# Projections of the second layer dealt as one stream over the token groups, and their weight preparation moved to ScalarE and GpSimd

## The chip, the cores and the metric

One NeuronCore of one Trainium2 chip. The metric is device time in microseconds (us) of the whole kernel. The kernel before takes 2705.66 us (median of three runs, 2705.16 to 2706.25). The engines are TensorE (PE for its matmuls, PEld for its weight loads), VectorE (DVE), ScalarE (ACT), GpSimd (POOL) and the queue of SyncE that issues the DMAs (SP).

## The reference, cut to what matters

Two layers over a sequence of 2048 tokens, 1024 features. The first is a gated linear attention. The second, which the change touches, is a stick-breaking attention of 16 heads of 64:

```
hk = rms_norm(x, kv_gain) * (1 + kv_scale) + kv_shift;  k, v = split(hk @ w_kv)
h  = rms_norm(x, gain)    * (1 + scale)    + shift;     q, g = split(h @ w_in)
z = q k^T * 64^-0.5                       # for each head, s < t only
log_beta = log_sigmoid(z);  log_one_minus = log_beta - z
w = exp(log_beta + reverse_cumsum(log_one_minus) - log_one_minus)
x = x + gate * ((w @ v) * silu(g)) @ w_out;   y = rms_norm(x, final_gain)
```

The norm's scale `a` and shift `b` are not applied to the tokens. They go into the weights: the projection uses `a * W` (one factor for each input feature) and adds the bias `b @ W`.

## The kernel before, in words

The sequence is cut into 4 token groups `g` of 512, the 16 heads into 8 pairs `p`. The normalised tokens lie in DRAM as a rounded part and a remainder (`xn_d`), and every product of the projections is three matmuls of 512 columns: high weight by high token, high by low, low by high (`mm3`, L143 to L153; the matmuls are L150, L151, L152).

**Projections.** `pair_linear(p, g)` (L732) computes v, k, q and the gate for one pair and one group, in this order. It is a generator: each `yield` follows the three matmuls of one of 8 slices of the features, so it has 4 times 8 steps and one more for its tail (`LIN_STEPS = 33`). It begins by loading eight tiles `xb` on SP. After each product ACT and DVE take the result out of PSUM.

**Weights.** `load_scaled` (L121) prepares a weight of 1024 by 256 in eight slices of 128 by 256, `kt` = 0 to 7. For each slice ACT writes the rounded `a * raw` (`hi`, L132), DVE the remainder (`lo`, L133), and DVE adds `b * raw` to a sum (`acc`, L138 for the first slice, L140 for the rest) from which TensorE later makes the bias (`pair_bias`, L720). A pair has two such weights, `w_kv` and `w_qg`, so 16 slices. `relaxed(n)` gives an instruction a priority that is n places later. The raw halves have three buffers, the prepared halves ten.

**Attention.** A `Unit` is one head, one query group and one key chunk of 512. It has four steps. `scores` makes z on TensorE (L821, L822), takes the sigmoid on ACT (L825) and runs the product scan on DVE (L830); in a chunk on the diagonal POOL first masks the last 128 columns (L827). `turn`, five steps later, transposes on TensorE (L838, four times) and splits into `sh` on ACT (L841) and `sl` on DVE (L842). `values`, some two steps after that, multiplies by v (L855, L856). Group g has 2(g+1) units, so 8, 16, 24 and 32 steps for g = 0 to 3.

**Order.** TensorE's order is that of the program text. The other engines' queues are put in order when the program is built, by a planner that takes ready instructions by priority. The loop of `layer1` (L964 on) runs the attention of one (pair, group) and fills each step with other work, by `step` (L956): during group g all 33 steps of the projection of group g+1, whatever g is; during group 3 those of the next pair's group 0. The weights `w_kv` of the next pair are dealt to the second half of group 2, `w_qg` to the first 60% of group 3. During group 3 of the last pair the fill is the final output projection.

The z banks and the transpose banks in PSUM are two each; the pool `m2` of 128 by 512 tiles (S, sh, sl and others) has 22 buffers, the token tiles 12.

Of the kernel before, what the change touches and what calls it, by code (L numbers as in the profile page):

```python
# [9 lines left out]
F32 = mybir.dt.float32  # L10
F32R = mybir.dt.float32r
AF = mybir.ActivationFunctionType
ALU = mybir.AluOpType
# [3 lines left out]
P = 128  # L17
D = 1024
KT = D // P
SEQ = 2048  # L20
TG = 512
NG = SEQ // TG
GH = 4
GV = 256
SBP = 8
# [9 lines left out]
def yoco_kernel(ctx: ExitStack, tc: tile.TileContext, I: dict, O: dict):  # L35
# [6 lines left out]
    nc = tc.nc  # L42
# [3 lines left out]
    wraw = ctx.enter_context(tc.tile_pool(name="wraw", bufs=3))  # L46
    wsp = ctx.enter_context(tc.tile_pool(name="wsp", bufs=10))
    m4 = ctx.enter_context(tc.tile_pool(name="m4", bufs=14))
    m2 = ctx.enter_context(tc.tile_pool(name="m2", bufs=22))
    pl = ctx.enter_context(tc.tile_pool(name="pl", bufs=4, space=PSUM))  # L50
    pz = ctx.enter_context(tc.tile_pool(name="pz", bufs=2, space=PSUM))
    pw = ctx.enter_context(tc.tile_pool(name="pw", bufs=2, space=PSUM))
# [3 lines left out]
    def t2(name, dt=F32):  # L56
        return m2.tile([P, TG], dt, tag="m2", name=name)
# [7 lines left out]
    def bank(pool, name):  # L65
# [9 lines left out]
                            fill=0.0, base=0, channel_multiplier=1)  # L75
# [45 lines left out]
    def load_scaled(name, src, out, mod, acc):  # L121


        a, b = mod
        for hf in range(2):
            raw, hi, lo = load_half(name, src, hf)
            out += [(hi[:, j], lo[:, j]) for j in range(4)]
            for j in range(4):
                kt = 4 * hf + j
                s = a[:, kt:kt + 1]  # L130
                with relaxed(100):
                    nc.scalar.activation(hi[:, j], raw[:, j], AF.Copy, scale=s)  # L132
                    nc.vector.scalar_tensor_tensor(lo[:, j], raw[:, j], s, hi[:, j].bitcast(F32),  # L133
                                                 op0=ALU.mult, op1=ALU.subtract)
                s = b[:, kt:kt + 1]
                with relaxed(400):
                    if kt == 0:
                        nc.vector.tensor_scalar(acc, raw[:, j], s, None, op0=ALU.mult)  # L138
                    else:
                        nc.vector.scalar_tensor_tensor(acc, raw[:, j], s, acc, op0=ALU.mult, op1=ALU.add)  # L140
                yield

    def mm3(out, w, blk, x, order=range(KT), first=True, last=True):  # L143
# [15 lines left out]
    def relaxed(n):  # L159

        return tc.high_priority(offset=-n) if n else nullcontext()
# [8 lines left out]
    def run(gen):  # L170
        for _ in gen:
            pass
# [535 lines left out]
    def new_weights(p):  # L708
        W = Piece()
        W.acc = t2(f"wacc_{p}").rearrange("p (i f) -> p i f", i=2)  # L710
        W.w, W.bias = {}, [None, None]
        return W

    def pair_weights(p, W, i):

        which, m = (("w_kv", "kvm"), ("w_qg", "l1m"))[i]
        W.w[which] = []
        return load_scaled(f"{which}{p}", I[which][p], W.w[which], mods[m], W.acc[:, i])
# [11 lines left out]
    LIN_STEPS = 4 * KT + 1  # L730
# [191 lines left out]

    LAG_T, LAG_V = 5, 2

    Ws = {}

    def prepare_pair(p):
# [4 lines left out]
    def layer1(after):  # L932
        Ls = {p: [] for p in range(SBP)}
        weave(pair_linear(0, 0, Ws[0], Ls[0]), (after, 0, 2))
        turns, values = [], []
        def final_all():

            seq = [final(g) for g in range(NG - 1)]
            seq += [final(NG - 1, i * TG // 2, TG // 2) for i in range(2)]
            for i, gen in enumerate(seq):  # L940
                ahead = final_inputs(i + 1) if i + 1 < NG else iter(())
                if i == 0:
                    yield from final_inputs(0)
                for j in range(FINAL_STEPS):
                    next(gen)
                    if i and j == (8 if i < 4 else 14):
                        run(seq[i - 1])
                    if j >= 32 and j % 4 == 0:
                        next(ahead, None)
                    yield  # L950
                run(ahead)
            run(seq[-1])

        finals = final_all()

        def step(gens, at):  # L956
            for f in gens:
                gen, n, f0, f1 = f[:4]
                want = min(n, int(n * (at - f0) / (f1 - f0) + 1e-6))
                while f[4] < want:  # L960
                    next(gen, None)
                    f[4] += 1

        for p in range(SBP):  # L964
            for g in range(NG):
                units = []
                for h in range(2):
                    before = None
                    for c in range(g, -1, -1):
                        before = Unit(p, g, h, c, Ls[p], before)  # L970
                        units.append(before)

                fill = [[after, 26, 0, 1, 0]] if p == 0 and g < 2 else []
                if p == SBP - 1 and g + 1 == NG:
                    fill.append([finals, FINAL_STEPS + SBP - 1, 0, 1.0, 0])
                elif g + 1 < NG:
                    fill.append([pair_linear(p, g + 1, Ws[p], Ls[p]), LIN_STEPS, 0, 1, 0])
                elif p + 1 < SBP:
                    fill.append([pair_weights(p + 1, Ws[p + 1], 1), KT, 0, 0.6, 0])
                    fill.append([pair_linear(p + 1, 0, Ws[p + 1], Ls[p + 1]), LIN_STEPS, 0, 1, 0])  # L980
                if g == 2 and p + 1 < SBP:
                    Ws[p + 1] = new_weights(p + 1)
                    fill.append([pair_weights(p + 1, Ws[p + 1], 0), KT, 0.5, 1, 0])
                steps = [(u, j) for u in units for j in range(4)]
                for i, (u, j) in enumerate(steps):
                    u.scores(j)
                    turns.append((u, j))
                    step(fill, (i + 0.7) / len(steps))
                    if len(values) > LAG_V:
                        v = values.pop(0)  # L990
                        v[0].values(v[1])
                    step(fill, (i + 1) / len(steps))
                    if len(turns) > LAG_T:
                        t = turns.pop(0)
                        t[0].turn(t[1])
                        values.append(t)
                for f in fill:
                    if f[0] is not finals and (f[0] is not after or g):
                        run(f[0])
        while turns or values:  # L1000
            for _ in range(3):
                next(finals)
            if turns:
                t = turns.pop(0)
                t[0].turn(t[1])
                values.append(t)
            for _ in range(3):
                next(finals)
            if len(values) > (LAG_V if turns else 0):
                v = values.pop(0)  # L1010
                v[0].values(v[1])
        run(finals)

    last = []
    play(layer0())
    layer1(last[0])


# [54 lines left out]
```

## Time and profile before

| | |
|---|---|
| median of three runs | 2705.66 us (2705.16 to 2706.25) |
| the profiled execution, its own time | 2703.88 us |
| its span, first to last instruction | 2702.1 us |
| PE busy | 2607.2 us, 96% |
| DVE busy | 2110.4 us, 78% |
| ACT busy | 1517.6 us, 56% |
| POOL busy | 167.4 us, 6% |
| mean granted TensorE clock | 0.989 of full |

Busy time is a union over the span, with issue and semaphore instructions left out. Matmuls overlap one another, so a matmul's duration is longer than the distance to the next one. The attention of the second layer begins at 976 us; pair 1 lies between 1170.5 and 1363.6 us, with its groups beginning at 1170.5, 1202.4, 1242.0 and 1296.8 us.

### The profile page before, as it was taken

The page shows a single profiled execution, that of the slowest core. Times are in us where ns is not written, and L with a number is a line of the kernel's source. Part 1 is how long each engine was busy: PE and PEld are TensorE (multiplying, and loading weights), DVE is VectorE, ACT ScalarE, POOL GpSimd, SP SyncE. Part 2 cuts the span into 40 slices and gives each one's busy share as a digit, 9 for nine tenths or more (in the row PEclk, how much of TensorE's full clock was granted, in tenths as well). Part 3 has the DMA queues.
Part 4 walks back from the last instruction along what each step waited for, and adds up shares of the span by engine and source line. Part 5 has one row for each costly group of instructions (what it writes and reads, how often), then busy time and mean ns, then how long its engine had stood idle before and what let it go on. Part 6 is the DMA issues. An engine that isn't in the chain of part 4 may idle for free.

```text
span 2702.1 us, 38165 instructions
## 1 busy us (share of the span) xinstructions
PE 2607.2 (96%) x14040; PEld 2184.4 (81%) x14040; DVE 2110.4 (78%) x2933; ACT 1517.6 (56%) x2677; POOL 167.4 (6%) x358
## 2 busy tenths in 40 slices
PE   5999999999999999999999999999999999999998
PEld 4888888888788878788787887887887887887887
DVE  7647767676675658978979969979879789789866
ACT  4746756574485445545545645546556555556644
POOL 3000000000000011000010010010000010010000
PEclk7999999999999999999999999999999999999999
DMA  6326445545732463342243334243243243323464
GB/s 246 118 74 209 151 151 175 168 148 173 232 131 72 164 247 127 106 145 90 96 146 116 114 107 154 88 137 116 75 148 110 72 151 113 115 93 117 148 212 147
DMA packets 116682, 371.91 MB, mean 138 GB/s; under 512 B 13872, under 2 KB 18096, under 8 KB 116496
## 3 DMA queue, kind: packets, MB, share of 16 engines
q1 hardware_dynamic: 116496, 369.47, 40.8%
q8 instruction: 111, 1.82, 0.3%
q14 instruction: 75, 0.61, 0.1%
HBM read 311.75 MB, written 40.89 MB: 131 GB/s over the span
## 4 chain that ended last, share of the span: by engine, by line
PE 75%; DVE 17%; ACT 3%; issue 3%; DMA 1%; POOL 0%; SPq 0%; DVEq 0%; POOLq 0%; ACTq 0%
PE pt L838 7%; DVE S L830 5%; PE z L822 4%; PE o L856 4%; PE z L821 4%; PE o L855 3%; DVE sl L842 3%; PE pg L150 2%; PE pg L152 2%; PE pg L151 2%; PE pf L150 2%; PE pf L151 2%; PE pf L152 2%; PE py L150 2%; PE lk L150 2%
## 5 line engine op out<-in xcount | busy, mean ns | idle before, releaser
L841 ACT ACTIVATE sh<-pt 128x512 fp32r<-128x512 f32 (+3 forms) x640 | 341.5, 534 | 531.7 <-PE pt L838 522.1
L842 DVE SCALAR_TENSOR_TENSOR sl<-pt,sh 128x512 fp32r<-128x512 f32 (+3 forms) x640 | 384.0, 601 | 163.5 <-ACT sh L841 157.6
L830 DVE TENSOR_TENSOR_SCAN S<-S,S 128x512 f32<-128x512 f32 x384 | 489.5, 1275 | 3.4 <-ACT S L825 3.0
L838 PE MATMUL pt<-ident,S 128*128 128x128 f32 x2176 | 346.9, 275 | 34.7 <-DVE sl L842 34.2
L838 PEld LDWEIGHTS pt<-ident,S 128*128 128x128 f32 x2176 | 266.1, 141 | 119.7 <-DVE sl L842 33.0
L825 ACT ACTIVATE S<-z 128x512 f32<-128x512 f32 (+3 forms) x640 | 339.5, 531 | 12.6 <-PE o L856 4.6
L821 PE MATMUL z<-k,q 128*128 128x512 f32 (+3 forms) x640 | 284.4, 444 | 0.0
L822 PE MATMUL z<-k,ql 128*128 128x512 f32 (+3 forms) x640 | 234.1, 366 | 0.9 <-DVE sl L842 0.5
L856 PE MATMUL o<-sl,v 128*128 128x512 f32 (+3 forms) x640 | 234.2, 366 | 0.0
L855 PE MATMUL o<-sh,v 128*128 128x512 f32 (+3 forms) x640 | 230.6, 360 | 0.0
L830 DVE TENSOR_TENSOR_SCAN S<-S 128x128 f32<-128x128 f32 (+3 forms) x256 | 209.3, 820 | 19.7 <-POOL S L827 16.7
L827 POOL TENSOR_SCALAR_AFFINE_SELECT S<-S 128x128 f32<-128x128 f32 x256 | 86.1, 337 | 1251.1 <-ACT S L825 1232.2
L444 PE MATMUL pv<-wh_v,h 128*128 128x256 f32 x512 | 155.0, 303 | 0.0
L446 PE MATMUL pv<-wh_v,h 128*128 128x256 f32 x512 | 145.3, 284 | 0.0
L445 PE MATMUL pv<-wl_v,h 128*128 128x256 f32 x512 | 145.2, 284 | 0.0
L855 PEld LDWEIGHTS o<-sh,v 128*128 128x128 f32 x640 | 120.6, 188 | 27.2
L856 PEld LDWEIGHTS o<-sl,v 128*128 128x128 f32 x640 | 120.6, 189 | 25.7
L821 PEld LDWEIGHTS z<-k,q 128*128 128x128 f32 x640 | 121.8, 190 | 5.5
L822 PEld LDWEIGHTS z<-k,ql 128*128 128x128 f32 x640 | 123.1, 192 | 1.5 <-DVE sl L842 0.7
L150 PE MATMUL pg<-h,wh_g 128*128 128x512 f32 x256 | 112.6, 440 | 0.0
L150 PE MATMUL lk<-xb,wh_w_kv 128*128 128x512 f32 x256 | 102.5, 400 | 7.6 <-DVE oB L869 7.6
L150 PE MATMUL lv<-xb,wh_w_kv 128*128 128x512 f32 x256 | 102.9, 402 | 3.5 <-DMA xb<-xn 3.5
(266 smaller groups left out, 6350.3 us busy)
## 6 DMA issues: line engine op xcount, KB each, us to landing
xb<-xn SPq DMA_DIRECT2D x256, 512.0 KB, 5.0
wa_l<-in_w_ada_dram SPq DMA_DIRECT2D x40, 512.0 KB, 5.2
wr_f<-in_w_out_dram SPq DMA_DIRECT2D x40, 512.0 KB, 3.8
x<-in_x_dram SPq DMA_DIRECT2D x32, 512.0 KB, 6.5
wr_v<-in_w_v_dram SPq DMA_DIRECT2D x32, 512.0 KB, 4.5
wr_kq<-in_w_kq_dram SPq DMA_DIRECT2D x32, 512.0 KB, 4.1
wr_g<-in_w_g_dram SPq DMA_DIRECT2D x32, 512.0 KB, 3.9
wr_out<-in_w_out_dram SPq DMA_DIRECT2D x32, 512.0 KB, 3.8
```

Of the source, the lines that this page charges most:

```text
L150: nc.tensor.matmul(out, hi, x[kt][0], start=first and i == 0, stop=False)
L444: nc.tensor.matmul(o, xh, hi, start=i == 0, stop=False)
L446: nc.tensor.matmul(o, xl, hi, start=False, stop=i == len(steps) - 1)
L821: nc.tensor.matmul(z, L.q[:, h, tcol], k[:, h, 0:w], start=True, stop=False)
L822: nc.tensor.matmul(z, L.ql[h][:, tcol], k[:, h, 0:w], start=False, stop=True)
L825: nc.scalar.activation(s, z, AF.Sigmoid, scale=-SCALE_B)
L830: nc.vector.tensor_tensor_scan(s[:, ::-1], s[:, ::-1], s[:, ::-1], 1.0 if diag else self.before.S[tb][:, 0:1], ALU.mult, ALU.min)
L838: nc.tensor.transpose(pt[:, tb * P:(tb + 1) * P], self.S[tb][:, sb * P:(sb + 1) * P], ident)
L841: nc.scalar.activation(hi, pt[:, t0 * P:], AF.Copy, bias=-1.0)
L842: nc.vector.scalar_tensor_tensor(lo, pt[:, t0 * P:], -1.0, hi.bitcast(F32), op0=ALU.add, op1=ALU.subtract)
L855: nc.tensor.matmul(o, v, hi, start=self.diag and sb == 0, stop=False)
L856: nc.tensor.matmul(o, v, lo, start=False, stop=self.c == 0 and sb == 3)
```

## The change

Two things change. The projections of all pairs become one generator, `projections()`, which the attention steps draw from by a running count `made`. At the end of group g of pair p the count must have reached `33 * (4p + g + 1)`, as before, and is let run ahead by `AHEAD[g]` of a projection; within a group the steps are dealt evenly. The weights of the next pair are drawn by every second step of the stream: `w_kv` from the middle of the projection (p, 3), `w_qg` from the start of (p+1, 0). In `load_scaled` all DVE instructions are gone: POOL makes the bias sum with a multiplication and an addition, ACT also scales the raw slice in place, and POOL subtracts. `m2` has one buffer less, and POOL gets two of 128 by 256.

```diff
-    m2 = ctx.enter_context(tc.tile_pool(name="m2", bufs=22))
+    m2 = ctx.enter_context(tc.tile_pool(name="m2", bufs=21))
+    wtmp = ctx.enter_context(tc.tile_pool(name="wtmp", bufs=2))
...
-                s = a[:, kt:kt + 1]
-                with relaxed(100):
-                    nc.scalar.activation(hi[:, j], raw[:, j], AF.Copy, scale=s)
-                    nc.vector.scalar_tensor_tensor(lo[:, j], raw[:, j], s, hi[:, j].bitcast(F32),
-                                                 op0=ALU.mult, op1=ALU.subtract)
-                s = b[:, kt:kt + 1]
                 with relaxed(400):
                     if kt == 0:
-                        nc.vector.tensor_scalar(acc, raw[:, j], s, None, op0=ALU.mult)
+                        nc.gpsimd.tensor_scalar(acc, raw[:, j], b[:, kt:kt + 1], None, op0=ALU.mult)
                     else:
-                        nc.vector.scalar_tensor_tensor(acc, raw[:, j], s, acc, op0=ALU.mult, op1=ALU.add)
+                        t = wtmp.tile([P, 256], F32, tag="wtmp", name=f"wt_{name}_{kt}")
+                        nc.gpsimd.tensor_scalar(t, raw[:, j], b[:, kt:kt + 1], None, op0=ALU.mult)
+                        nc.gpsimd.tensor_tensor(acc, acc, t, op=ALU.add)
+                with relaxed(100):
+                    s = a[:, kt:kt + 1]
+                    nc.scalar.activation(hi[:, j], raw[:, j], AF.Copy, scale=s)
+                    nc.scalar.activation(raw[:, j], raw[:, j], AF.Copy, scale=s)
+                    nc.gpsimd.tensor_tensor(lo[:, j], raw[:, j], hi[:, j].bitcast(F32), op=ALU.subtract)
                 yield
...
+    AHEAD = (0.1, 0.0, 0.15, 0.6)
...
+        def projections():
+            for p in range(SBP):
+                for g in range(NG):
+                    side, start, every = iter(()), 0, 2
+                    if g == 0:
+                        if p == 0:
+                            continue
+                        side = pair_weights(p, Ws[p], 1)
+                    elif g == NG - 1 and p + 1 < SBP:
+                        Ws[p + 1] = new_weights(p + 1)
+                        side, start = pair_weights(p + 1, Ws[p + 1], 0), LIN_STEPS // 2
+                    for i, _ in enumerate(pair_linear(p, g, Ws[p], Ls[p])):
+                        if i >= start and (i - start) % every == 0:
+                            next(side, None)
+                        yield
+                    run(side)
+                    yield
+        stream = projections()
+        made = [0]
+        def project(n):
+            while made[0] < n and next(stream, 0) is None:
+                made[0] += 1
...
-                elif g + 1 < NG:
-                    fill.append([pair_linear(p, g + 1, Ws[p], Ls[p]), LIN_STEPS, 0, 1, 0])
-                elif p + 1 < SBP:
-                    fill.append([pair_weights(p + 1, Ws[p + 1], 1), KT, 0, 0.6, 0])
-                    fill.append([pair_linear(p + 1, 0, Ws[p + 1], Ls[p + 1]), LIN_STEPS, 0, 1, 0])
-                if g == 2 and p + 1 < SBP:
-                    Ws[p + 1] = new_weights(p + 1)
-                    fill.append([pair_weights(p + 1, Ws[p + 1], 0), KT, 0.5, 1, 0])
+                n0, n1 = made[0], int(LIN_STEPS * (NG * p + g + 1 + AHEAD[g]))
                 steps = [(u, j) for u in units for j in range(4)]
+                def go(at):
+                    step(fill, at)
+                    project(n0 + int(at * (n1 - n0) + 1e-6))
                 for i, (u, j) in enumerate(steps):
...
-                    step(fill, (i + 0.7) / len(steps))
+                    go((i + 0.7) / len(steps))
...
-                    step(fill, (i + 1) / len(steps))
+                    go((i + 1) / len(steps))
...
+                project(LIN_STEPS * (NG * p + g + 1))
```

## Rows read from the trace of the kernel before

**Rows 1.** The page: busy time of engines, and the chain that ended last, by engine.
```profile
PE 2607.2 (96%) x14040; PEld 2184.4 (81%) x14040; DVE 2110.4 (78%) x2933; ACT 1517.6 (56%) x2677; POOL 167.4 (6%) x358
...
PE 75%; DVE 17%; ACT 3%; issue 3%; DMA 1%; POOL 0%; SPq 0%; DVEq 0%; POOLq 0%; ACTq 0%
```
**Rows 2.** Windows, pairs 1 and 6 and the end: stretch, length, busy of PE, PEld, DVE, ACT, POOL.
```profile
1170.50:1363.60 193.10, 187.83 (x1003) 155.50 (x1001) 166.50 (x235) 106.89 (x213) 15.04 (x40) 1.00 0.35 115
...
2136.00:2328.80 192.80, 187.83 (x1003) 155.54 (x1002) 166.25 (x232) 106.33 (x210) 16.09 (x40) 1.00 0.36 118
...
2456.70:2702.00 245.30, 229.82 (x1252) 196.24 (x1250) 190.98 (x264) 127.79 (x197) 4.47 (x8) 0.98 0.48 159
```
**Rows 3.** Windows, groups 0 to 3 of pair 1.
```profile
1170.50:1202.40 31.90, 31.90 (x164) 26.57 (x162) 17.68 (x25) 11.97 (x24) 3.70 (x10) 1.00 0.25 71
1202.40:1242.00 39.60, 39.60 (x213) 33.25 (x212) 32.26 (x44) 20.39 (x41) 4.06 (x10) 1.00 0.49 168
1242.00:1296.80 54.80, 51.96 (x281) 42.41 (x279) 51.72 (x81) 34.84 (x71) 3.71 (x10) 1.00 0.34 113
1296.80:1363.60 66.80, 64.36 (x354) 53.28 (x353) 64.84 (x88) 39.69 (x78) 3.57 (x10) 1.00 0.31 107
```
**Rows 4.** Windows, pair 1: the stretch of its weight preparation, and one behind it.
```profile
1260.00:1304.00 44.00, 39.86 (x212) 31.47 (x211) 43.66 (x73) 27.20 (x57) 2.39 (x7) 1.00 0.45 150
...
1318.00:1364.00 46.00, 46.00 (x259) 38.82 (x258) 44.18 (x56) 28.58 (x55) 2.07 (x6) 1.00 0.30 98
```
**Rows 5.** Waits of PE, from 1260 to 1304 us: total us, times, longest.
```profile
PE pt L838 <- DVE sl L842: 4.1, 7, 1.2
```
**Rows 6.** Waits of PE, pair 0 (976 to 1170.5 us): total us, times, longest.
```profile
PE pt L838 <- DVE sl L842: 4.0, 7, 1.2
PE lv L150 <- DMA xb<-xn: 3.5, 1, 3.5
PE lk L150 <- DVE oB L869: 1.1, 1, 1.1
```
**Rows 7.** Groups by line, 1260 to 1304 us: count, busy us, mean ns, idle before.
```profile
L830 DVE TENSOR_TENSOR_SCAN S<-S,S 128x512 f32<-128x512 f32 x12 | 15.3, 1272 | 0.0
L842 DVE SCALAR_TENSOR_TENSOR sl<-pt,sh 128x512 fp32r<-128x512 f32 (+3 forms) x18 | 10.8, 597 | 0.1
...
L133 DVE SCALAR_TENSOR_TENSOR wl_w_qg<-wr_w_qg,a_l,wh_w_qg 128x256 fp32r<-128x256 f32 x8 | 3.7, 471 | 0.0
```
**Rows 8.** Windows, 1260 to 1304 us, the instructions on the bias sum alone.
```profile
1260.00:1304.00 44.00, 0.00 (x0) 0.00 (x0) 6.94 (x16) 1.00 0.45 150
```
**Rows 9.** Weight preparation by line, whole span: ns min/median/max.
```profile
L132 ACT ACTIVATE wh_w_kv<-wr_w_kv,a_kv x64: 493/500/512, 911.9 to 2227.8; 128x256 fp32r<-128x256 f32 x64
...
L133 DVE SCALAR_TENSOR_TENSOR wl_w_kv<-wr_w_kv,a_kv,wh_w_kv x64: 452/464/480, 914.2 to 2230.3; 128x256 fp32r<-128x256 f32 x64
...
L140 DVE SCALAR_TENSOR_TENSOR wacc<-wr_w_kv,cond_kv,wacc x56: 454/469/486, 918.3 to 2249.9; 128x256 f32<-128x256 f32 x56
```
**Rows 10.** Timeline: three projection matmuls lie between these two starts.
```profile
1320.27 0.40 PE L150 MATMUL lk<-xb,wh_w_kv 128*128 128x512 f32 x1
...
1320.97 0.28 PE L855 MATMUL o<-sh,v 128*128 128x256 f32 x1
```
**Rows 11.** POOL, and DVE beside it, by line: ns min/median/max, first and last start.
```profile
L323 POOL TENSOR_TENSOR x<-x,r_x x8: 1714/2240/2248, 20.5 to 35.4; 128x512 f32<-128x512 f32 x8
...
L341 POOL TENSOR_SCALAR xn<-x,a_l,cond_l x4: 1188/1718/2076, 44.2 to 49.2; 128x512 f32<-128x512 f32 x4
...
L827 POOL TENSOR_SCALAR_AFFINE_SELECT S<-S x256: 291/295/1894, 977.4 to 2511.5; 128x128 f32<-128x128 f32 x128
...
L482 POOL TENSOR_SCALAR_AFFINE_SELECT sc<-sc x16: 637/638/1620, 88.8 to 877.9; 128x512 f32<-128x512 f32 x16
...
L244 DVE SCALAR_TENSOR_TENSOR aa_l<-wa_l,s_col,aa_l x35: 1273/1285/2177, 12.0 to 726.0; 128x1024 f32<-128x1024 f32 x35
```
**Rows 12.** Waits of SP's queue in pair 1: total us, times, longest.
```profile
SPq L106 <- DVE wacc L140: 22.2, 2, 16.4
```

## The prediction

> **What bounds the kernel now.** I read the page first. TensorE is 96% busy and holds 75% of the chain, VectorE holds 17% [rows 1]. That is a mean, so I cut the second layer into its pairs. Pair 1 lasts 193.1 us, and TensorE is busy in 187.83 of them; pair 6 is 192.8 with the same 187.83, and the four between are as pair 1 within 0.1 us [rows 2]. So a pair has 5.27 us in which TensorE stands still. No re-dealing of TensorE's own work can give more than that, as long as its matmuls cost what they cost.
>
> Then the groups. In groups 0 and 1 TensorE is never idle and VectorE is busy for 17.7 of 31.9 and 32.3 of 39.6 us. In groups 2 and 3 TensorE loses 2.84 and 2.44 us and VectorE is 94% and 97% busy [rows 3]. The idle time lies in one place: from 1260 to 1304 us VectorE works 43.66 of 44 us and TensorE 39.86; from 1318 to 1364 TensorE works all 46 us while VectorE, at 96%, just keeps up [rows 4]. In the first stretch TensorE waits seven times for `sl`, 4.1 us [rows 5]. What sets that stretch apart is the weights: the bias sum takes 6.94 us there [rows 8] and the eight remainders of `w_qg` 3.7 [rows 7]. So the bound is TensorE nearly everywhere, and VectorE for some 44 us of each pair, because the weights of the next pair are prepared on it.
>
> **The change, part by part.** *The stream.* Three projection matmuls take 1320.97 - 1320.27 = 0.70 us [rows 10], so the 33 steps of a projection take 23.1 us. Taken from TensorE's busy time in rows 3, attention alone is 8.8, 16.5, 28.9 and 41.3 us for groups 0 to 3. The new counts follow from 33(4p+g+1+AHEAD): 17, 30, 37 and 48 steps, 132 as before. Group times with TensorE full: 8.8+11.9 = 20.7, 16.5+21.0 = 37.5, 28.9+25.9 = 54.8, 41.3+33.6 = 74.9; in all 187.9 us. The stream by itself removes no work. It makes groups 0 and 1 shorter and group 3 longer, so that VectorE has more TensorE time beside it where it was late.
>
> *Weights off VectorE.* A pair loses 16 remainders of 0.46 to 0.47 us and 16 sums of about 0.47 [rows 9]: 15.0 us. VectorE's 166.5 us [rows 2] become 151.5 of 187.9.
>
> *Weights on POOL.* 16 multiplications, 14 additions and 16 subtractions of 128x256 for a pair. No row shows these at that width. The nearest with two inputs is 128x512: beside it a VectorE sum of 1285 ns takes up to 2177, so POOL held it up by 0.89 us [rows 11]. The mask takes 295 ns for 128 columns and 638 for 512, so some 409 or 0.64 of the latter for 256 [rows 11]; I take 0.64 x 0.89 = 0.57 us (bounds 0.45, half, and 0.89, all of it). For the multiplication with one input I take the mask's 0.41 (upper bound half of the fastest 1188 ns, 0.59). Sum 16 x 0.41 + 30 x 0.57 = 23.7 us, on an engine that is busy 15.0 of 193 us [rows 2].
>
> *What POOL does to VectorE.* The scan reads SBUF twice and takes 1272 ns; `sl` (full width some 0.68, mean of all forms 597 ns) reads its main input from PSUM [rows 7]. POOL's own mask took up to 1894 ns instead of 295 [rows 11]. So I count that a POOL instruction waits for a running scan, and then holds up the next. If two of them (0.41 + 0.57) start as a scan ends, `sl` covers 0.68 of it and the next scan is 0.30 us late: 0.15 for each, 7 us for 46. Bounds: 0 (all under `sl`) and 23.7 (all in front of a scan).
>
> Is there room? The stretch of rows 4 has 18 steps [rows 7]. Of VectorE's 43.66 us at most 43.66 - 6.94 - 3.7 = 33.0 stay. TensorE did 22.2 + 3.6 projection steps there (33 x 36.8/54.8 and 33 x 7.2/66.8); for the same attention it will do 24.8 + 5.2, so 4.2 more: 39.86 + 2.9 = 42.8 us. VectorE gets seven evacuations of some 0.7 us for 33 steps, 0.6 us more: 33.6. Room: 9.2 us. 7 fit into it, 23.7 don't.
>
> The Trainium skill, "SBUF — State Buffer", section "Who interferes with whom", speaks against this edit: a VectorE instruction with two SBUF inputs and a GpSimd one that reads SBUF exclude each other, and whichever begins first keeps the port to its end. The 1285 to 2177 ns above bear that out. By the rule at its worst the 23.7 us count in full; by the cover of `sl`, 7.
>
> *ScalarE* gets 16 scalings in place at 0.50 us [rows 9], 8.0 us a pair: in the stretch 27.2 + 8.0 = 35.2 of 42.8. A new wait comes with it: the scaling overwrites the raw slice, so it must wait for POOL's multiplication of that slice. Behind it in ScalarE's queue stand the sigmoids and `sh`, and for these wait the scan and, with two z banks, TensorE. One such wait is at most a scan and an addition, 1.27 + 0.57 = 1.84 us; ScalarE's idle time (7.6 us over 16) hides 0.47. Upper bound 16 x 1.37 = 22 us a pair, lower bound 0, since the planner can put it where the slice is long done. I take 1 us a pair for this and for what is left of the waits, a quarter of the 4.1 us that a full VectorE cost, and keep both ends.
>
> *At nothing:* SP now waits 22.2 us in a pair for the bias sum to release a raw buffer [rows 12], with the `xb` loads behind it, and TensorE does not wait for a load there [rows 5]; POOL's subtraction releases it instead. If that cover went, one late `xb` costs the 3.5 us of pair 0 [rows 6]. One `m2` buffer less: the tiles of the next projection come earlier in group 3 and a sigmoid may wait for a slot; 0, at most a scan's 1.27 us for each of the last eight steps, 10 us a pair. Pair 0's own weights are made at the end of the first layer, from 912 us on [rows 9]; the same 23.7 us of POOL end some 936, before attention begins at 976: 0, and at most the 3.5 us of a late load. The last group (245.3 us [rows 2]) has no projections and keeps its time.
>
> *Sum.* Pairs 1 to 5 regain 5.27 each, pair 6 4.97 [rows 2], pair 0 the 4.0 + 1.1 for `sl` and a bank, not the 3.5 for a load [rows 6]: 36.4 us. Less 7 x 1: 29.4. The profiled execution took 2703.88, so 2674.5; the median shown is 1.78 above it: 2676.
>
> **Rivals.** *Slower: the shared port.* The mechanism above with its cover gone: the planner packs POOL's instructions in front of scans. It decides where the delay passes the room and the old idle time, 9.2 + 5.3 = 14.5 us, 0.32 us for each of 46. At 0.42 the stall is 19.3 - 9.2 = 10.1, so 4.8 a pair worse, 7 x 4.8 = 34: 2739. All 23.7: 14.5 - 5.3 = 9.2, 2770. For it: VectorE was stretched in every case of a long POOL instruction. Against: in rows 4 VectorE has `sl` after each scan.
>
> *Slower: ScalarE parked behind POOL.* From 0.33 us of TensorE's time for each of the 16 waits on. Half of the upper bound, 11 - 5.3 = 5.7 a pair: 2746. For it: ScalarE at 82% has little to hide it. Against: POOL is idle 92% of the time, so multiplications can run early.
>
> *The gain is half eaten.* 0.26 us for each POOL instruction: 12 - 9.2 + 1 = 3.8 of 5.3 stay: 2705.7 - 7 x 1.5 = 2695.
>
> *No change.* VectorE at 96% beside a full TensorE [rows 4] says the scans alone are near the bound; with the port at 0.30 us the old idle time comes back as a new one: 2700 to 2711.
>
> **How the numbers follow.** This kernel's measurement tells 0.2%, 5.4 us, from no change. Forecast 0.58 (its own range 2664, with pair 0's load gone too, to 2690, at 3 us left a pair); half eaten 0.13; no change 0.10; port 0.12; parked 0.07. Faster 0.58 + 0.13 = 0.71, same 0.10, slower 0.19. The range goes from 2662 to 2716, which leaves out most of the slower cases and a few hundredths below.
>
> **What would show it.** Right: each of pairs 1 to 6 near 189 us; groups near 21, 38, 55 and 75; the waits of TensorE for `sl` nearly gone; VectorE some 15 us less a pair; POOL 25 to 60 more, for its instructions wait inside their spans. The port: scans well over 1285 ns and TensorE waiting for `sl` again in groups 2 and 3. Parked: ScalarE waiting for `wt` or the sum, and TensorE's z for ScalarE. The prediction is wrong if TensorE's busy time in a pair rises over 188, or if its idle time stays at 5 us.

## The result, and the profile after

| | before | after |
|---|---|---|
| median of the comparison | 2705.41 us (4 runs, 2704.99 to 2706.25) | 2803.64 us (4 runs, 2802.28 to 2807.76) |
| profiled execution / its span | 2703.88 / 2702.1 us | 2803.85 / 2802.1 us |
| mean granted TensorE clock | 0.989 | 0.969 |

The ratio is 1.0365, 95% interval 1.0347 to 1.0383: slower by 3.65%, where 2676 us and a range to 2716 had been predicted.

The page of the changed kernel: busy time of the engines, then the chain that ended last (it answers to [rows 1]).
```profile
PE 2633.7 (94%) x14040; PEld 2210.5 (79%) x14040; DVE 2046.9 (73%) x2677; ACT 1575.9 (56%) x2805; POOL 492.9 (18%) x726
...
PE 78%; POOL 8%; DVE 6%; ACT 3%; issue 2%; DMA 2%; SPq 0%; POOLq 0%; DVEq 0%; ACTq 0%
```
GpSimd held 0% of the chain of before and holds 8% here, though it is busy only 18% of the span. It is the share of the chain, not the share of the span, that this case turns on.

Windows of the changed kernel, columns as in rows 2 (behind the five busy times stand the granted clock, the DMA share and GB/s): groups 0 to 3 of pair 1, the whole pair, and a stretch inside group 2.
```profile
1198.50:1219.50 21.00, 21.00 (x117) 17.64 (x115) 16.00 (x23) 10.74 (x21) 2.73 (x8) 1.00 0.58 207
1219.50:1257.10 37.60, 37.60 (x205) 31.55 (x202) 30.68 (x43) 19.82 (x40) 4.01 (x10) 1.00 0.30 106
1257.10:1332.60 75.50, 59.65 (x293) 48.62 (x290) 49.65 (x61) 43.10 (x91) 43.78 (x56) 0.89 0.32 114
1332.60:1406.60 74.00, 74.00 (x399) 61.87 (x398) 62.96 (x79) 40.55 (x76) 5.42 (x12) 1.00 0.21 72
1198.50:1406.60 208.10, 192.25 (x1003) 159.69 (x1002) 159.29 (x203) 114.21 (x228) 55.94 (x86) 0.96 0.30 107
1280.00:1325.00 45.00, 29.14 (x128) 23.06 (x127) 22.69 (x25) 23.49 (x51) 36.33 (x46) 0.81 0.27 87
```
Against [rows 3], groups 0, 1 and 3 have TensorE busy throughout and last 21.0, 37.6 and 74.0 us, where 20.7, 37.5 and 74.9 were predicted. Group 2 lasts 75.5 instead of 54.8. In the 45 us from 1280 GpSimd is busy for 36.33, and TensorE for 29.14, VectorE for 22.69 and ScalarE for 23.49: none of those three is the bound there.

The same group of pairs 0 and 6, and group 2 of pair 7, in which GpSimd has no weights to prepare.
```profile
1049.10:1124.50 75.40, 59.59 (x293) 48.52 (x291) 49.64 (x61) 43.09 (x91) 43.77 (x56) 0.89 0.33 116
2294.70:2367.10 72.40, 58.40 (x292) 47.48 (x290) 49.00 (x60) 41.63 (x86) 43.33 (x52) 0.91 0.33 115
2501.80:2558.10 56.30, 52.85 (x279) 43.80 (x278) 54.44 (x72) 39.67 (x74) 4.86 (x10) 0.96 0.37 113
```
With weights on GpSimd the group takes 72.4 to 75.5 us in all seven pairs, without them 56.3.

Waits of all engines in group 2 of pair 1: total us, times, longest (against [rows 5]).
```profile
DVE S L832 <- POOL S L829: 22.0, 5, 8.7
PE pt L840 <- DVE sl L844: 15.9, 4, 8.3
...
ACT wr_w_kv L141 <- POOL wt_w_kv L136: 5.2, 3, 1.9
```
TensorE's 15.9 us are all for `sl`, as before, but `sl` is late for another reason. VectorE's scan (L832) waits for the mask that GpSimd puts on a diagonal chunk (L829). GpSimd's timeline around one such wait (start us, duration us, engine, line, operation, tiles):
```profile
1290.00 0.29 POOL L829 TENSOR_SCALAR_AFFINE_SELECT S<-S 128x128 f32<-128x128 f32 x1
1290.26 0.73 POOL L142 TENSOR_TENSOR wl_w_kv<-wr_w_kv,wh_w_kv 128x256 fp32r<-128x256 f32 x1
1290.94 0.85 POOL L137 TENSOR_TENSOR wacc<-wacc,wt_w_kv 128x256 f32<-128x256 f32 x1
...
1292.45 0.92 POOL L136 TENSOR_SCALAR wt_w_kv<-wr_w_kv,cond_kv 128x256 f32<-128x256 f32 x1
...
1299.58 0.72 POOL L137 TENSOR_TENSOR wacc<-wacc,wt_w_qg 128x256 f32<-128x256 f32 x1
1300.26 0.29 POOL L829 TENSOR_SCALAR_AFFINE_SELECT S<-S 128x128 f32<-128x128 f32 x1
```
VectorE at the same time; in brackets the idle time before an instruction and whom it waited for:
```profile
1290.32 0.94 DVE L832 TENSOR_TENSOR_SCAN S<-S 128x128 f32<-128x128 f32 x1 [4.22 <-POOL S L829]
1291.19 0.66 DVE L844 SCALAR_TENSOR_TENSOR sl<-pt,sh 128x512 fp32r<-128x512 f32 x1
1300.58 1.20 DVE L832 TENSOR_TENSOR_SCAN S<-S 128x256 f32<-128x256 f32 x1 [8.73 <-POOL S L829]
```
The sigmoid of ScalarE that the second mask had to wait for:
```profile
1291.37 0.37 ACT L827 ACTIVATE S<-z 128x256 f32<-128x256 f32 x1
```
Between two masks of 0.29 us stand thirteen weight instructions in GpSimd's queue. The second mask's input is ready at 1291.74, and the mask starts at 1300.26. VectorE stands still for 8.73 us until it is through. No shared resource is needed to explain it: GpSimd works with no gap over 0.1 us, in the order that its queue has.

The new groups on GpSimd over the whole span, count, then ns min/median/max (they answer to [rows 9, 11]).
```profile
L136 POOL TENSOR_SCALAR wt_w_kv<-wr_w_kv,cond_kv x56: 916/924/1882, 899.4 to 2330.0; 128x256 f32<-128x256 f32 x56
...
L142 POOL TENSOR_TENSOR wl_w_kv<-wr_w_kv,wh_w_kv x64: 714/728/1486, 915.0 to 2338.0; 128x256 fp32r<-128x256 f32 x64
...
L137 POOL TENSOR_TENSOR wacc<-wacc,wt_w_kv x56: 718/737/1574, 903.3 to 2331.8; 128x256 f32<-128x256 f32 x56
```
A pair's work on GpSimd is 16 x 0.92 + 30 x 0.73 = 36.6 us. These are the durations without contention: several in the timeline above have them while VectorE stands still. In pair 1 the 46 instructions take some 41 us, with those that were stretched.

### The profile page after: what moved, and what is told of

It is laid out like the page before. It is cut to its first block, busy times and chain, and to the rows that moved or that the text cites. A ratio compares the mean times of both kernels' runs of the same rounds, so it can differ in the third digit from the quotient of the medians.

```text
span 2802.1 us, 38570 instructions
## 1 busy us (share of the span) xinstructions
PE 2633.7 (94%) x14040; PEld 2210.5 (79%) x14040; DVE 2046.9 (73%) x2677; ACT 1575.9 (56%) x2805; POOL 492.9 (18%) x726
## 4 chain that ended last, share of the span: by engine, by line
PE 78%; POOL 8%; DVE 6%; ACT 3%; issue 2%; DMA 2%; SPq 0%; POOLq 0%; DVEq 0%; ACTq 0%
PE pt L840 7%; PE o L858 4%; PE z L824 4%; PE z L823 4%; PE o L857 4%; POOL wacc L137 3%; PE pg L152 2%; PE lv L152 2%; PE pg L154 2%; PE pg L153 2%; PE pf L152 2%; PE pf L153 2%; PE pf L154 2%; PE lv L153 2%; PE lv L154 2%
## 5 line engine op out<-in xcount | busy, mean ns | idle before, releaser
L832 DVE TENSOR_TENSOR_SCAN S<-S,S 128x512 f32<-128x512 f32 x384 | 496.0, 1292 | 21.7 <-ACT S L827 19.8
L840 PEld LDWEIGHTS pt<-ident,S 128*128 128x128 f32 x2176 | 274.9, 143 | 196.4 <-DVE sl L844 91.8
L832 DVE TENSOR_TENSOR_SCAN S<-S 128x128 f32<-128x128 f32 (+3 forms) x256 | 224.2, 879 | 170.1 <-POOL S L829 166.8
L829 POOL TENSOR_SCALAR_AFFINE_SELECT S<-S 128x128 f32<-128x128 f32 x256 | 84.4, 330 | 970.3 <-ACT S L827 970.2
L484 POOL TENSOR_SCALAR_AFFINE_SELECT sc<-sc 128x512 f32<-128x512 f32 x16 | 11.6, 726 | 816.4 <-ACT sc L482 695.6
L152 PE MATMUL lg<-xb,wh_w_qg 128*128 128x512 f32 x256 | 111.4, 435 | 0.0
```

What stands on the lines that cost most here:

```text
L152: nc.tensor.matmul(out, hi, x[kt][0], start=first and i == 0, stop=False)
L832: nc.vector.tensor_tensor_scan(s[:, ::-1], s[:, ::-1], s[:, ::-1], 1.0 if diag else self.before.S[tb][:, 0:1], ALU.mult, ALU.min)
L840: nc.tensor.transpose(pt[:, tb * P:(tb + 1) * P], self.S[tb][:, sb * P:(sb + 1) * P], ident)
```

## The experiments

The theory: the queue. GpSimd executes its instructions in the order of its queue, the masks of group 2 stand behind the weights, and VectorE and then TensorE wait for the masks. Rivals: the port (GpSimd's instructions stretch VectorE's), parked (ScalarE's scaling in place waits for GpSimd's multiplication, with `sh` behind it), and the stream itself. Line numbers shift by a few between kernels. Ratios are to the kernel before, run beside each.

**1. The stream alone** (e1), the weights as before.
```diff
-                        nc.gpsimd.tensor_tensor(acc, acc, t, op=ALU.add)
...
-                    nc.scalar.activation(raw[:, j], raw[:, j], AF.Copy, scale=s)
-                    nc.gpsimd.tensor_tensor(lo[:, j], raw[:, j], hi[:, j].bitcast(F32), op=ALU.subtract)
+                    nc.vector.scalar_tensor_tensor(lo[:, j], raw[:, j], s, hi[:, j].bitcast(F32),
+                                                 op0=ALU.mult, op1=ALU.subtract)
...
+                        nc.vector.scalar_tensor_tensor(acc, raw[:, j], s, acc, op0=ALU.mult, op1=ALU.add)
```


> Only the stream; the weights are prepared on VectorE as before. All theories (mask queue, shared port, ScalarE parked) lay the loss to POOL's new instructions, so the loss of 98 us must go: groups 0, 1 and 3 stay near 21, 37.5 and 74 us, group 2 falls from 75 to 57 to 60 (VectorE needs some 46 us in a stretch where TensorE needs 42.8, so about 3 us of TensorE's idle time stay in a pair instead of 5.3). Total 2680 to 2695. If it stays above 2760, the stream is to blame.

Measured: 2690.35 us against 2702.25, 0.9955 (0.9939 to 0.9970). Windows: group 2 and the whole of pair 1.
```profile
1242.30:1300.30 58.00, 55.81 (x292) 46.02 (x290) 55.12 (x86) 34.67 (x71) 4.05 (x10) 0.97 0.39 138
...
1183.70:1374.60 190.90, 188.58 (x1003) 157.09 (x1002) 167.79 (x235) 107.41 (x212) 16.59 (x40) 0.99 0.33 116
```
Total and group 2 are as expected. The stream gains: 190.9 us a pair against 193.1, although `m2` has one buffer less here too. VectorE is busy for 55.12 of the 58.0 us of group 2, which is what is left of the old bound.

**2. The weights alone** (e2), the projections dealt as before: the whole of `projections()` taken out, the calls of before put back.
```diff
-                n0, n1 = made[0], int(LIN_STEPS * (NG * p + g + 1 + AHEAD[g]))
...
+                    fill.append([pair_linear(p, g + 1, Ws[p], Ls[p]), LIN_STEPS, 0, 1, 0])
...
+                    fill.append([pair_weights(p + 1, Ws[p + 1], 0), KT, 0.5, 1, 0])
```


> Only the weight preparation moves to ScalarE and GpSimd; the projections are dealt as before. If the loss is POOL's alone, by its queue or by the port, it appears here too: in a pair 15 to 25 us of TensorE's idle time where before had 5.3, total 2775 to 2845. If the loss needs the stream (its later dealing of the weights), it is within 30 us of before.

Measured: 2775.89 us, 1.0270 (1.0250 to 1.0289). Group 2 of pair 1:
```profile
1250.80:1315.30 64.50, 54.82 (x279) 45.07 (x277) 46.46 (x58) 40.20 (x85) 40.27 (x47) 0.89 0.22 71
```
VectorE's longest wait in it:
```profile
DVE S L832 <- POOL S L829: 11.4, 3, 5.8
```
The move of the weights by itself loses 74 us, and the wait for the mask is here too. The stream is absent, so the loss does not need it; with the stream it is 25 us larger.

**3. Four masks of each pair off GpSimd** (e3b): those of the second head in group 2 (32 of 256) are made on VectorE, as a maximum with a constant tile; all 46 weight instructions stay on GpSimd.
```diff
+                if self.g == 2 and h == 1:
+                    nc.vector.tensor_tensor(s[:, w - P:], s[:, w - P:], masks[:, 0, 0:2 * P].bitcast(F32), op=ALU.max)
+                else:
```


> The changed kernel, with the four masks of the second head in group 2 (32 of the 256) made on VectorE as a maximum with a constant tile, about 0.2 to 0.3 us each; all of POOL's weight instructions stay. Mask queue: these masks stood in POOL's queue behind six to ten weight instructions, so group 2 falls from 75 to 55 to 59 us and the total to 2675 to 2705. Shared port or ScalarE parked: the 46 weight instructions of a pair and their port time are the same, so group 2 stays above 70 and the total above 2770.

Measured: 2714.61 us against 2702.25, 1.0047 (1.0031 to 1.0063). Group 2 of pair 1:
```profile
1240.70:1301.10 60.40, 55.01 (x293) 44.61 (x291) 48.97 (x63) 41.17 (x89) 40.89 (x46) 1.00 0.36 127
```
The largest waits of VectorE and TensorE in it, and the longer of ScalarE's two for GpSimd (the other, for `wt_w_qg`, is 3.3 us):
```profile
DVE sl L847 <- ACT sh L846: 8.3, 8, 4.2
PE pt L843 <- DVE sl L847: 5.4, 5, 1.8
ACT wr_w_kv L141 <- POOL wt_w_kv L136: 5.3, 4, 1.9
```
This is the deciding run. GpSimd has as many weight instructions in a pair as in the changed kernel, VectorE has four maxima more, and group 2 falls from 75.5 to 60.4 us, the total by 89. Both expectations missed the total: it is 10 us above the 2705 of the queue and 55 below the 2770 of the rivals. But the port as a cause of the large loss falls with it. The scans' wait for the mask is gone from the list, and the next one appears, which explains why the queue's range was missed: ScalarE's scaling waits for GpSimd. ScalarE's timeline:
```profile
1270.39 0.51 ACT L141 ACTIVATE wr_w_kv<-wr_w_kv,a_kv 128x256 f32<-128x256 f32 x1 [1.94 <-POOL wt_w_kv L136]
...
1273.71 0.51 ACT L141 ACTIVATE wr_w_kv<-wr_w_kv,a_kv 128x256 f32<-128x256 f32 x1 [1.60 <-POOL wt_w_kv L136]
1274.12 0.58 ACT L846 ACTIVATE sh<-pt 128x512 fp32r<-128x512 f32 x1
```
The VectorE instruction that waits for this `sh`:
```profile
1274.73 0.69 DVE L847 SCALAR_TENSOR_TENSOR sl<-pt,sh 128x512 fp32r<-128x512 f32 x1 [4.22 <-ACT sh L846]
```
The `sh` that TensorE's next step needs stands behind two parked scalings, and `sl` is 4.22 us late. That is the predicted rival "ScalarE parked".

**4. All 256 masks on VectorE.** (e3)
```diff
-                nc.gpsimd.affine_select(s[:, w - P:], s[:, w - P:], pattern=[[-1, P]],
...
+                nc.vector.tensor_tensor(s[:, w - P:], s[:, w - P:], masks[:, 0, 0:2 * P].bitcast(F32), op=ALU.max)
```


> As the run with the four masks of group 2's second head on VectorE, but with all 256 masks there, so that POOL has no mask at all. If those four were the whole of the queue's harm, this is within 8 us of that run (2714.6; VectorE has 28 more maxima of 0.3 to 0.5 us in a pair, which groups 0 and 3 hide). If masks elsewhere still wait behind weights, it is 10 to 25 us faster.

Measured: 2708.24 us against 2703.65, 1.0013 (1.0004 to 1.0023). Group 2 lasts 60.3 us and group 3 74.0. As expected for the case that the four were the whole harm, the total is within 8 us of run 3. The other 224 masks are worth 7.8 us against run 3 by their differences to the kernel before (12.4 and 4.6): the four were nearly all of it.

**5. Less work on GpSimd: the bias sum back on VectorE** (e4), all masks left on GpSimd, which keeps 16 subtractions a pair.
```diff
-                        nc.gpsimd.tensor_tensor(acc, acc, t, op=ALU.add)
+                        nc.vector.scalar_tensor_tensor(acc, raw[:, j], s, acc, op0=ALU.mult, op1=ALU.add)
```


> The changed kernel, with the bias sum back on VectorE: POOL keeps 16 subtractions of 46 instructions in a pair (about 12 of 37 us), VectorE gets 7.5 us back. Mask queue: what stands before a mask falls to about a third, so group 2 loses 5 to 8 us instead of 21: 2710 to 2735. Shared port: the stall goes with the port time, likewise to a third, 2705 to 2735; this run tells how the loss scales with POOL's work, not which of the two it is. ScalarE parked: its wait for the multiplication is now one for VectorE; above 2770 only if that wait was the cause.

Measured: 2698.13 us against 2702.25, 0.9987 (0.9978 to 0.9997), better than the 2710 to 2735 that were expected. Group 2 of pair 1, and the scans' wait for the masks in it:
```profile
1243.90:1302.90 59.00, 54.65 (x291) 44.49 (x290) 54.88 (x76) 42.65 (x91) 17.80 (x26) 1.00 0.40 139
...
DVE S L831 <- POOL S L828: 0.8, 4, 0.3
```
With GpSimd at 17.80 us instead of 43.78 the masks are in time although they stand in the same queue: a backlog is needed, not just company. VectorE is back at 54.88 of 59.0.

**6. The other half: the sum on GpSimd, the remainders on VectorE, no scaling in place** (e5), with the four masks of run 3.
```diff
-                    nc.scalar.activation(raw[:, j], raw[:, j], AF.Copy, scale=s)
-                    nc.gpsimd.tensor_tensor(lo[:, j], raw[:, j], hi[:, j].bitcast(F32), op=ALU.subtract)
+                    nc.vector.scalar_tensor_tensor(lo[:, j], raw[:, j], s, hi[:, j].bitcast(F32),
+                                                   op0=ALU.mult, op1=ALU.subtract)
```


> As the run with the four masks on VectorE, with the remainders back on VectorE too (16 of 0.47 us a pair) and ScalarE's scaling in place gone; POOL keeps the bias sum, 30 of 46 instructions. That run left 5.6 us of group 2 over 54.8. If ScalarE parked behind POOL's multiplications makes them, group 2 falls to 55 to 57.5 and the total to 2680 to 2697, although VectorE has 7.5 us more. If the shared port makes them, group 2 stays at 59 to 61 (two thirds of the port time stays, and VectorE has more to do) and the total above 2705.

Measured: 2694.36 us against 2703.65, 0.9967 (0.9955 to 0.9978). Group 2 lasts 56.5 us in pair 1 and up to 57.8 in the others; the total is in the range for "parked". With neither the four masks nor ScalarE behind GpSimd, 30 weight instructions a pair on it (36.74 us busy in group 2) leave group 2 within 1.7 to 3.0 us of the predicted 54.8.

**7. ScalarE waits for nobody** (e6): run 3, and the sum is taken from the scaled slice, times b/a, after the scaling; so the raw slice may be overwritten at once.
```diff
+    def over(m):
+        r = m2.tile([P, KT], F32, tag='bl', name='rcp', bufs=2)
+        nc.vector.reciprocal(r, m[0])
+        nc.vector.tensor_tensor(m[1], m[1], r, op=ALU.mult)
...
+                    nc.scalar.activation(raw[:, j], raw[:, j], AF.Copy, scale=s)
+                    nc.gpsimd.tensor_tensor(lo[:, j], raw[:, j], hi[:, j].bitcast(F32), op=ALU.subtract)
                 with relaxed(400):
```


> As the run with the four masks on VectorE, with the sum taken from the scaled slice times b/a, so that POOL waits for ScalarE and ScalarE for nobody; POOL's 46 instructions stay. ScalarE parked: group 2 from 60.4 to 55 to 57.5, total 2714.6 to 2680 to 2700. Shared port: group 2 stays at 59 to 61, total within 8 us of 2714.6.

Measured: 2730.55 us against 2703.65, 1.0104 (1.0089 to 1.0119). Groups 2 and 3 of pair 1:
```profile
1252.30:1307.10 54.80, 53.89 (x292) 45.04 (x290) 51.41 (x66) 42.76 (x92) 37.76 (x37) 1.00 0.23 76
1307.10:1388.70 81.60, 76.13 (x398) 63.23 (x398) 61.69 (x78) 40.23 (x75) 17.08 (x28) 0.96 0.34 119
```
The waits of VectorE and TensorE in group 3, and SP's for GpSimd in both groups:
```profile
DVE S L842 <- POOL S L839: 12.0, 2, 11.8
PE z L831 <- DMA ql<-ql: 5.3, 1, 5.3
...
SPq L107 <- POOL wt_w_kv L141: 19.5, 2, 10.2
```
Group 2 is at the predicted 54.8 at last, and ScalarE no longer waits for GpSimd in it: the 5.6 us behind the masks went with the parked ScalarE. (GpSimd also does fewer of its instructions within group 2, 37 of all kinds where run 3 does 46; what that gives was not separated.) But group 3 now takes 81.6 instead of 74.0, and the total is above both ranges. TensorE waits for `ql`, a small copy that SP issues. SP's timeline:
```profile
1292.02 10.11 SPq L107 DMA_DIRECT2D wr_w_kv<-in_w_kv_dram  x2
1302.23 0.47 SPq L792 DMA_DIRECT2D q<-q  x1
1304.60 0.47 SPq L792 DMA_DIRECT2D ql<-ql  x1
```
The load of the next raw slices waits at the head of SP's queue until GpSimd has released the buffer, 10.11 us, and the `ql` copies, whose data VectorE had finished by 1292.70, stand behind it. They also land late, 8.0 us after their issue where the run's median is 2.6, in a stretch in which the DMA engines are full: the loads that stood behind the same wait come all at once. This run changes the order of the sum in the plan too, so its two differences are not wholly pure.

**8. Run 7 with all masks on VectorE** (e8): is group 3 late for the masks (12.0 us) or for `ql`?
```diff
-                if self.g == 2 and h == 1:
-                    nc.vector.tensor_tensor(s[:, w - P:], s[:, w - P:], masks[:, 0, 0:2 * P].bitcast(F32), op=ALU.max)
-                else:
...
+                nc.vector.tensor_tensor(s[:, w - P:], s[:, w - P:], masks[:, 0, 0:2 * P].bitcast(F32), op=ALU.max)
```


> As the run with the sum from the scaled slice (2730.6, group 2 at 54.8 but group 3 at 81.6), with all masks on VectorE. There a mask of group 3 waited 11.8 us on POOL and z waited 5.3 us for a copy of ql that stood on SP behind a raw load waiting 10 us for POOL. If queues are the cause: the mask's part of group 3's 7.6 us goes, the ql part stays: group 3 at 77 to 80, total 2700 to 2720. If the port is: group 3 stays above 81, total 2725 to 2735.

Measured: 2727.83 us against 2703.25, 1.0097 (1.0080 to 1.0113). Group 3 stays at 82.5 us. Both are in the ranges expected for the port, not for the queues, but the only wait of TensorE in group 3 is that for `ql`, 5.7 us. So the masks of group 3 are not it. Of VectorE's 11.8 us in run 7 the first half came from the late `ql` (the sigmoid before the mask ended at 1313.51), the second from GpSimd's queue (the mask began at 1319.09), and taking the second away changed nothing for TensorE.

**9. Run 8 with the raw loads issued from GpSimd's queue** (e9), so that SP no longer waits there; the loads for the final projection, from pair 6 on, stay on SP.
```diff
-        nc.sync.dma_start(raw, src[:, 4 * hf:4 * hf + 4, :])
+        q.dma_start(raw, src[:, 4 * hf:4 * hf + 4, :])
...
+            raw, hi, lo = load_half(name, src, hf, nc.gpsimd)
```


> As the one with sum from the scaled slice and all masks on VectorE, with the raw loads of the layer-2 weights issued from POOL's own queue, so that no other engine's queue holds an instruction behind POOL's weight work. All of POOL's 46 instructions and their port time stay. Queues: groups near 21, 38, 55 and 74 to 75 us as predicted, total 2675 to 2690. Port: no better than 2705.

Measured: 2725.54 us, 1.0080 (1.0064 to 1.0095), again in the range expected for the port. Group 3 of pair 1 is back at 74.0 us, and it is 74.0 to 75.2 in pairs 0 to 5, so SP's queue was the cause there. In pair 6 it is still 83.5. There SP still holds such a load, and TensorE waits for `ql` again:
```profile
2263.42 14.00 SPq L107 DMA_DIRECT2D wr_f<-in_w_out_dram  x2
...
PE z L831 <- DMA ql<-ql: 6.9, 1, 6.9
```
But group 2 is 61.5, and the waits in it name the next queue:
```profile
ACT wh_w_kv L133 <- DMA wr_w_kv<-in_w_kv_dram: 6.9, 1, 6.9
PE pt L846 <- DVE sl L850: 4.9, 2, 4.5
```
GpSimd issues the load at 1297.98 us, among its own instructions; it lands 7.0 us later, and ScalarE waits 6.9 us for it, with `sh` behind. VectorE's scans take 95.58 us in pair 1 here, against 87.32 in run 1; how much of the loss that is left comes from them, by the port or otherwise, was not separated.

**10. Run 6 with all masks on VectorE and the raw loads on GpSimd.** (e10)
```diff
-                if self.g == 2 and h == 1:
...
-            raw, hi, lo = load_half(name, src, hf)
+            raw, hi, lo = load_half(name, src, hf, nc.gpsimd)
```


> The sum on POOL, the remainders on VectorE, all masks on VectorE, raw loads from POOL's queue. The run like it with loads on SP and only four masks moved took 2694 (groups 20.9, 37.6, 56.4, 75.2). Queues: group 3 falls to 74, group 2 keeps 1 to 2 us because VectorE is 95% busy there: 2680 to 2690. If the remaining 2 us a pair are VectorE's work alone, no change: 2690 to 2698.

Measured: 2702.99 us, 0.9999 (0.9990 to 1.0009): as the kernel before, outside both expectations and some 9 us slower than run 6. Group 2 of pair 1 lasts 57.0 us, in the other pairs 57.8 to 61.2. Why the two moves lose here was not shown.

**11. The stream alone with more of it in group 2** (e7) (`AHEAD[2]` 0.3 for 0.15).
```diff
-    AHEAD = (0.1, 0.0, 0.15, 0.6)
+    AHEAD = (0.1, 0.0, 0.3, 0.6)
```


> The stream alone, weights on VectorE, with AHEAD 0.3 in place of 0.15 for group 2: five projection steps (3.5 us of TensorE) move from group 3 to group 2, where VectorE keeps TensorE waiting some 2.3 us. If that idle time can be filled: group 2 58 to 59 to 60, group 3 74.3 to 71, 1 to 2 us a pair less than the stream alone, 2676 to 2684. If the projections' own evacuations on VectorE (some 0.7 us more) or the weights that come with the stream eat it: 2688 to 2696.

Measured: 2694.64 us against 2703.65, 0.9971 (0.9962 to 0.9981), no better than run 1, as expected for the case that the gain is eaten. Group 3 shrinks by 3.6 us to 70.7, and group 2 grows by as much, to 61.6 us. TensorE still waits 2.6 us there for `sl`, as it did 2.0 in run 1: the added steps did not fill the idle time. VectorE is busy for 58.26 of the 61.6 us, so its own load is the likely reason; no run tests it alone.

**12. The stream alone with its weights at lower priority** (e12) (100 to 300, 400 to 800).
```diff
-                with relaxed(100):
+                with relaxed(300):
...
-                with relaxed(400):
+                with relaxed(800):
```


> The stream alone, weights on VectorE (2690, 0.9955 of before; groups 20.9, 37.6, 58.0, 74.4), with their priority put further back (rounded part and remainder 300 places, sum 800). If the planner then moves them from group 2, where VectorE is 95% busy, to group 3, where it is 89%, group 2 falls to 55 to 56.5 with group 3 at 74.4: 2672 to 2684. If they come too late, TensorE waits for the bias sum or a remainder in group 3: group 3 above 76, total 2690 or more. If the planner's order doesn't change much: 2688 to 2693.

Measured: 2688.29 us against 2703.26, 0.9945 (0.9931 to 0.9959), as expected for the case that the order changes little. The group times are those of run 1, and the difference to it is inside the intervals. These two have the lowest ratios; runs 5, 6 and 11 are also faster than the kernel before, by 0.1 to 0.3%.

## Why the prediction was wrong

**The step that failed** is "Weights on POOL", in its last clause: 23.7 us "on an engine that is busy 15.0 of 193 us". It weighed the new work against GpSimd's idle share of a pair and asked what GpSimd does to VectorE by the port and to ScalarE by the multiplication. It did not ask what stands behind the new instructions in GpSimd's own queue. Among those 15.0 us are the masks, and each stands between a sigmoid and a scan for which TensorE waits. The new instructions come in bunches, and a mask that falls into one waits for all that stand before it, whatever the mean: 22.0 us of VectorE's waits in group 2 of pair 1, 15.9 of TensorE's. Taking four masks of a pair off that queue gave back 15.1 of the 20.7 us that group 2 was too long (run 3).

**Sizes.** The multiplication was taken as 0.41 us (upper bound 0.59) and is 0.92; additions and subtractions, taken as 0.57 (0.45 to 0.89), are 0.73. So 36.6 us and not 23.7, and the backlog in front of a mask is half as long again. The upper bound for the multiplication halved the duration of a row of twice the width; the multiplication takes 0.92 us where that row takes 1.188, so 77% of the time for half the width. With the right sizes the prediction would still have missed the queue.

**The clock.** Of the 20.7 us, 75.5 - 59.65 = 15.85 are TensorE standing still. The other 4.85 are TensorE's own busy time, 59.65 instead of 54.8. In the stretch from 1280 to 1325 us, where TensorE is busy for 29.14 of 45, the granted clock is 0.81, a mixture of the full 2.4 GHz and the 1.2 GHz level. Two pieces of it:
```profile
1298.00:1300.00 2.00, 0.00 (x0) 0.00 (x0) 0.00 (x0) 0.82 (x2) 1.92 (x3) 0.50 0.00 0
...
1304.00:1306.00 2.00, 2.00 (x6) 1.52 (x6) 0.00 (x0) 1.93 (x4) 1.92 (x4) 0.50 0.42 156
```
TensorE stands still for 8.26 us until 1302.42; within that wait the clock falls to half, and it is still half while TensorE works again. In groups 0, 1 and 3 it is 1.00. In run 3, where TensorE's longest wait in group 2 is 1.8 us, it is 1.00 there too. An idle TensorE paid a second time, which the prediction had not counted in any rival, though it named a busy time over 188 us in a pair as a sign of being wrong; it is 192.25.

**"ScalarE parked"** was priced at 1 us a pair and given 0.07, with the argument "Against: POOL is idle 92% of the time, so multiplications can run early." The same mean as above. It measures some 5.6 us (60.4 to 54.8, runs 3 and 7), a quarter of the rival's upper bound of 22 us and half of the 11 that its price of 5.7 net starts from, but hidden behind the masks in the changed kernel.

**"At nothing: SP".** In the changed kernel it cost nothing that can be seen. SP's waits in pair 1 (against [rows 12]):
```profile
SPq L107 <- POOL wl_w_kv L142: 15.9, 2, 9.5
...
SPq L107 <- ACT wr_w_kv L141: 7.8, 1, 7.8
```
When the masks and ScalarE were out of the way it was 7.6 us in pair 1 (81.6 against 74.0, runs 7 and 9): 5.5 us in which TensorE stands still, and 2.1 of longer busy time at a clock of 0.96. The prediction looked at the `xb` loads behind the waiting load; it was the `ql` copies that were late.

**What held.** The stream's own terms: group times within 1 us in three groups, and a gain by itself (run 1), though 2.2 us a pair and not the 5.27 that the whole change was to bring. VectorE's busy time is 159.29 us a pair, where 151.5 plus 7 for the port were predicted, but that agreement is luck. Of VectorE's instructions it is the scans that were stretched: they take 90.33 us in pair 1 against 87.32 in run 1, so 3.0 us. Part of the other 4.8 is that less goes with the weights than 15.0 us: in run 1 they cover 13.84 us of the pair, since neighbouring instructions overlap in the record. What makes up the remainder is not shown. GpSimd's own instructions were stretched by more, some 41 us in pair 1 instead of 36.6. So the port's 3.0 us stayed inside the room of 9.2 that the prediction gave it. The Trainium skill, "SBUF — State Buffer", section "Who interferes with whom", says that a VectorE instruction with two SBUF inputs contends with a GpSimd instruction that reads SBUF, and that the shared port is an exclusive lock. The trace agrees in kind: single multiplications on GpSimd take up to 1882 ns instead of 924.

**The sum again.** Group 2 lasts 522.5 us in pairs 0 to 6 together, where 7 x 54.8 = 383.6 were predicted: 139 too long. The predicted 2674.5 holds 7 us for waits on top of groups with a full TensorE; against those, 2667.5, the profiled execution is 136.4 too long. Group 3, 0.9 shorter seven times, gives 6 back, and some 3 to 4 are lost elsewhere. By its own terms the prediction's 2664 comes out as some 2666, on which nothing hangs.

**Still open.** Why the planner put thirteen weight instructions between two masks: whether its durations for GpSimd are too short, or its priorities let them pass, was not measured. The halves don't add up either: runs 1 and 2 give -11.9 + 73.6 = 61.7 us, the whole change 98.2. In group 2 of pair 1 the move of the weights costs 64.5 - 54.8 = 9.7 us without the stream and 75.5 - 58.0 = 17.5 with it, so the difference lies there; GpSimd's work in group 2 is denser with the stream (43.78 us against 40.27 in run 2), but that this makes the rest was not shown. Nor was a version tried that holds the weights back by hand until each mask is issued. Runs 8 and 9 ended in the ranges expected for the port; their traces name other waits, but the port's part in them was not separated.

## What to carry to other kernels

Before an instruction is moved to an idle engine, list what stands behind it in that engine's queue and who waits for that; the idle share says nothing where the new work comes in bunches. A wait taken out of one in-order queue shows the next: here the masks on GpSimd, then `sh` on ScalarE, then `ql` on SP, each behind the same slow work. Moving four masks took the loss from 98 to 12 us, but with all 46 weight instructions on GpSimd no version came out faster than the kernel before; two of the three with fewer did (runs 5 and 6, not 10). And a kernel that changes two things is first run as each half: one half here gains 0.45%, the other loses 2.7%.

## What the runs showed of the hardware

A GpSimd multiplication of 128x256 by a factor for each partition takes 0.92 us, longer than an addition of two such tiles, 0.73, with one input less to read; the mask of half the width takes 0.29. On VectorE the multiplication and addition together take 0.47 [rows 9].
